# Adaptive max pooling: the short first load as four DMAs

## The chip, the cores and the metric

The kernel runs on 1 core of one Trainium2 chip. The metric is device time in microseconds (us), the median of several runs; lower is better. The profile shows one execution of the program. Its span goes from the first to the last instruction of the core and is shorter than the device time. Engines in the profile: DVE is VectorE, ACT is ScalarE, POOL is GpSimd, SP is SyncE; a letter q behind a name (SPq) means that engine's sequencer, which issues DMAs and waits.

## What is computed

The input x is 32 x 256 x 4096 float32 (134 MB), the output 32 x 256 x 256. Each output is the maximum of 16 neighbouring inputs:

```
for i in range(output_size):          # 256
    start = int(i * length / output_size)
    end = int((i + 1) * length / output_size)
    result[:, :, i] = np.max(x[:, :, start:end], axis=-1)
```

## The kernel before

All windows of 16 inputs form one long list of 2,097,152 windows, 16,384 for each of the 128 partitions. The list is cut into two groups, A and B; in each, a partition owns one contiguous run of windows in HBM, so a load of n windows reads, for each partition, one contiguous row of n x 64 bytes. A load of 1024 windows is 128 rows of 64 KB, 8 MiB in all.

Group A has 10 loads: a short one of 128 windows (FIRST, line 38; 128 rows of 8 KB, 1 MiB), eight of 1024 and one of 1020. Group B has six of 1024 and a last one of 900. All are issued by SyncE, in program order: the short one on line 87, the others on line 96. Within group A the loads go from the end of each partition's run to its start, in group B from start to end.

They land in one buffer, `ring` (line 48), of 2 x (1024 + 152) windows per partition. The short load goes to windows 1024 to 1151. The large loads alternate between the lower and the upper half, and within a half alternately at offset 0 and at offset 152 (GAP). Two loads that follow each other in a half so overlap in all but 152 windows. The reduction of a large load is split accordingly on VectorE (`pooled`, line 54 to 60, called on lines 99 to 101): first a part of 872 windows, which is what the next load in this half overwrites, then the other 152. The next load of the half waits for the first part and is issued while the second part and the other half's load are still going on. The third large load, at windows 152 to 1175 of the lower half, overwrites the short load's place too, so it also waits for the short load's reduction (line 90).

Reductions write into `kept` (line 49), 15,484 windows per partition. The last load's maxima stay in `ring`; ScalarE stores them from there (line 114). SyncE stores the rest in two DMAs behind all the loads (line 117). The framework assigns semaphores and places the waits; each DMA adds to one of eight semaphores in rotation, and a load's reduction waits for that one.

Of the kernel before, what the change touches and what calls it, by code (L numbers as in the profile page):

```python
# [1 line left out]

# [4 lines left out]


@with_exitstack
def kernel(  # L10
    ctx: ExitStack,
    tc: tile.TileContext,
    x: bass.AP,
    output_size: bass.AP,
    out: bass.AP,
):

    nc = tc.nc
    P = nc.NUM_PARTITIONS
    fp32 = mybir.dt.float32

    B, C, L = x.shape
    O = int(output_size)  # L30
    assert L % O == 0, (L, O)
    W = L // O
    total = B * C * O // P
    assert B * C * O % P == 0

    CHUNK = 1024
    GAP = 152
    FIRST = 128
    LOADS_A, LOADS_B = 9, 6

    LESS = 4
    group_a = [FIRST] + [CHUNK] * (LOADS_A - 1) + [CHUNK - LESS]
    last = total - sum(group_a) - LOADS_B * CHUNK
    group_b = [CHUNK] * LOADS_B + [last]
    assert 0 < last and last * (W + 1) <= CHUNK * W

    pool = ctx.enter_context(tc.tile_pool(name="pool", bufs=1))
    ring = pool.tile([P, 2 * (CHUNK + GAP) * W], fp32, tag="ring", name="ring")
    kept = pool.tile([P, total - last], fp32, tag="kept", name="kept")

    xw = x.flatten_outer_dims().rearrange("r (o w) -> (r o) w", w=W)
    ow = out.flatten_outer_dims().rearrange("r o -> (r o)")

    def pooled(dst, at, n):

        nc.vector.reduce_max(  # L56
            out=dst,
            in_=ring[:, at * W : (at + n) * W].rearrange("p (n w) -> p n w", w=W),
            axis=mybir.AxisListType.X,
        )  # L60

    taken = 0

    def group(n):

        nonlocal taken
        span = slice(taken * P, (taken + n) * P)
        taken += n
        return (
            xw[span].rearrange("(p n) w -> p (n w)", p=P),  # L70
            ow[span].rearrange("(p n) -> p n", p=P),
        )

    stores = []
    n_loads = 0
    base = 0
    for g, loads in enumerate((group_a, group_b)):
        xg, og = group(sum(loads))
        a = sum(loads) if g == 0 else 0
        for n in loads:  # L80
            if g == 0:
                a -= n
            xn = xg[:, a * W : (a + n) * W]
            dst = kept[:, base + a : base + a + n] if n != last else None
            if n == FIRST:

                nc.sync.dma_start(  # L87
                    out=ring[:, CHUNK * W : (CHUNK + n) * W], in_=xn
                )
                pooled(dst, CHUNK, n)  # L90
            else:

                low = n_loads % 2 * (CHUNK + GAP)
                moved = n_loads // 2 % 2
                at = low + moved * GAP
                nc.sync.dma_start(out=ring[:, at * W : (at + n) * W], in_=xn)
                if n != last:
                    cut = CHUNK - GAP if moved else GAP
                    parts = [(0, cut), (cut, n)]
                    for u, v in parts if moved else parts[::-1]:  # L100
                        pooled(dst[:, u:v], at + u, v - u)
                else:
                    end = (at + CHUNK) * W
                    last_kept = ring[:, end - n : end]
                    pooled(last_kept, at, n)
                n_loads += 1
            if g:
                a += n
        full = a - last if g else sum(loads)
        stores.append((og[:, 0:full], kept[:, base : base + full]))  # L110
        base += full
    assert taken == total

    nc.scalar.dma_start(out=og[:, full : full + last], in_=last_kept)
    tc.no_sync_barrier()
    for dst, src in stores:
        nc.sync.dma_start(out=dst, in_=src)


# [1 line left out]
_INS = ['x', 'output_size']  # L121
_OUTS = [((32, 256, 256), 'float32')]

_NUMBERS = {'output_size': 256}


# [26 lines left out]
```

## Time and profile before

| what | value |
|---|---|
| device time, median of 3 runs | 335.07 us (334.96 to 335.25) |
| span of the profiled execution | 333.1 us (its own device time is not listed apart; against the median, 2.0 us lie around the span) |
| instructions in the profile | 113 |
| DMA packets, bytes | 2880 packets, 142.61 MB |
| HBM read, written | 134.22 MB, 8.39 MB |
| mean rate over the span | 428 GB/s |
| issue of the short load on SyncE | 0.383 us, from 0.73 us |
| reduction of the short load | 2.29 us, from 5.44 us |
| reduction of 872 windows | 14.69 us each (14 of them) |
| reduction of 152 windows | 2.68 us each (15 of them) |
| reduction of the last load, 900 windows | 15.14 us, from 312.82 us |
| issue of the last store, on ScalarE | at 327.99 us |

How to read it: a DMA is issued by an engine's sequencer, then runs on the core's 16 DMA engines, and lands when all of them have added to its semaphore. A load's packet is one row of a partition (8 KB or 64 KB); besides, each of the 16 engines writes a small end marker per DMA, which counts as a packet too: 19 DMAs on SyncE's queue with 128 rows each make 2432 rows and 304 markers, the 2736 packets that the page gives for that queue. The chain of work goes back from the last instruction, at each step to what released it. The idle time before an instruction is put down to what ended it.

### The profile page before, as it was taken

The numbers are of one execution on the slowest core, as the hardware profiler recorded it, in microseconds if no ns is written. First come the engines' busy times: TensorE is split into PE (matmuls) and PEld (weight loads), VectorE is DVE, ScalarE is ACT, GpSimd is POOL, SyncE is SP. The second block draws the span as 40 slices with busy tenths as digits, with TensorE's granted clock in tenths as the row PEclk, the third lists the DMA queues.
The fourth block names the chain that finished last, engine by engine and source line by source line (L and its number), as shares of the span: only waits on it lengthen the run. The fifth ranks groups of instructions, "written<-read, shape, count | busy, mean of one in ns | idle before, by whom it ended". The sixth has DMA issues, their size and how long they took to land.

```text
span 333.1 us, 113 instructions
## 1 busy us (share of the span) xinstructions
DVE 276.5 (83%) x32; POOL 0.2 (0%) x4
## 2 busy tenths in 40 slices
DVE  2009979797997979799797979979797998979993
POOL 0000000000000000000000000000000000000000
DMA  9898989899898989899898989899898989899997
GB/s 378 378 504 378 504 378 504 378 449 433 378 504 378 504 378 504 378 441 441 384 494 377 504 378 504 378 456 425 386 496 378 504 378 504 378 458 443 393 395 330
DMA packets 2880, 142.61 MB, mean 428 GB/s; under 512 B 320, under 2 KB 320, under 8 KB 448
## 3 DMA queue, kind: packets, MB, share of 16 engines
q1 hardware_dynamic: 2736, 142.15, 98.8%
q10 hardware_dynamic: 144, 0.46, 0.3%
HBM read 134.22 MB, written 8.39 MB: 428 GB/s over the span
## 4 chain that ended last, share of the span: by engine, by line
DMA 57%; DVE 36%; DVEq 5%; issue 0%; SPq 0%
DMA ring<-in_x_dram 57%; DVE kept L56 36%; DVEq L148 5%; SPq L87 0%
## 5 line engine op out<-in xcount | busy, mean ns | idle before, releaser
L56 DVE TENSOR_REDUCE kept<-ring 128x152 f32<-128x2432 f32 (+3 forms) x31 | 261.4, 8473 | 51.5 <-DMA ring<-in_x_dram 51.5
L56 DVE TENSOR_REDUCE ring<-ring 128x900 f32<-128x14400 f32 x1 | 15.1, 15143 | 0.0
L134 POOL MEMSET const-bfloat16-1.0<- 128x1 bf16 x1 | 0.1, 103 | 0.0
L134 POOL MEMSET const-uint8-127<- 128x1 uint8 x1 | 0.1, 102 | 0.0
L134 POOL MEMSET const-float32-0.0<- 128x1 f32 x1 | 0.1, 100 | 0.2 <-issue 0.2
L134 POOL MEMSET const-float32-1.0<- 128x1 f32 x1 | 0.1, 99 | 0.0
## 6 DMA issues: line engine op xcount, KB each, us to landing
ring<-in_x_dram SPq DMA_DIRECT2D x1, 8160.0 KB, 23.9
ring<-in_x_dram SPq DMA_DIRECT2D x1, 7200.0 KB, 21.7
out_dram<-kept SPq DMA_DIRECT2D x1, 4670.0 KB, 32.4
out_dram<-kept SPq DMA_DIRECT2D x1, 3072.0 KB, 18.2
ring<-in_x_dram SPq DMA_DIRECT2D x1, 1024.0 KB, 4.7
out_dram<-ring ACTq DMA_DIRECT2D x1, 450.0 KB, 4.2
ring<-in_x_dram SPq DMA_DIRECT2D x14, 24.0
```

Of the source, the lines that this page charges most:

```text
L56: nc.vector.reduce_max(out=dst, in_=ring[:, at * W : (at + n) * W].rearrange("p (n w) -> p n w", w=W), axis=mybir.AxisListType.X,)
L134: nc = _bacc.Bacc("TRN2", target_bir_lowering=False, num_devices=1)
L148: with _tile.TileContext(nc) as tc:
```

## The change

The short load is no longer one DMA over 128 partitions but four over 32 partitions each, all issued from SyncE one after another. Share s holds the partitions s, s + 4, s + 8 and so on; each row is the same 8 KB from the same address to the same place as before. The reduction of the short load is one instruction as before and waits for all four. The order of instructions on VectorE, ScalarE and GpSimd is unchanged; on SyncE, four DMAs stand where one stood, ahead of all others. The semaphores of the later DMAs shift by three places in their rotation.

```
+    SHARES = 4
...
             if n == FIRST:
 
-                nc.sync.dma_start(
-                    out=ring[:, CHUNK * W : (CHUNK + n) * W], in_=xn
-                )
+                for s in range(SHARES):
+                    nc.sync.dma_start(
+                        out=ring[s:P:SHARES, CHUNK * W : (CHUNK + n) * W],
+                        in_=xn[s:P:SHARES, :],
+                    )
                 pooled(dst, CHUNK, n)
```

## The prediction

> **What bounds the kernel now.** I read the page first, then the chain of work in order of time, SyncE's own waits, and two cuts into stretches: the first microseconds and the end.
>
> The page, busy shares, queues, the chain's shares and the DMA issues:
> ```profile
> DVE 276.5 (83%) x32; POOL 0.2 (0%) x4
> ...
> q1 hardware_dynamic: 2736, 142.15, 98.8%
> ...
> DMA 57%; DVE 36%; DVEq 5%; issue 0%; SPq 0%
> ...
> ring<-in_x_dram SPq DMA_DIRECT2D x1, 1024.0 KB, 4.7
> ```
> VectorE is idle for a sixth of the span, while the 16 DMA engines are taken for 98.8% of it by SyncE's queue. The last line is the load that the change cuts up: 4.7 us from issue to landing.
>
> The chain, from its start (start us, us, what):
> ```profile
> 0.73 0.38 SPq L87
> 1.11 0.05 issue
> 1.16 23.59 DMA ring<-in_x_dram
> 24.76 0.02 issue
> 24.78 14.70 DVE kept L56
> 39.48 0.02 issue
> 39.49 23.96 DMA ring<-in_x_dram
> 63.45 0.02 issue
> 63.48 14.70 DVE kept L56
> ```
> The chain alternates between a load and the reduction that frees its place. It looks like a loop through VectorE, and is not one that decides: the load issued at 39.49 takes 23.96 us, but the load ahead of it lands only at 44.13 (the reduction of it starts there in the timeline). So it stands in the queue for 4.6 us, and the engines never run dry. One 8 MiB load lands every 19.35 us (63.48 - 44.13), that is 433.5 GB/s, and each reduction pair takes 17.28 us, so VectorE then waits 2.07 us for the next landing.
>
> Stretches (us, length, VectorE busy, POOL busy, clock, DMA share, GB/s), the start and then the rest:
> ```profile
> 1.60:1.80 0.20, 0.00 (x0) 0.00 (x0) 1.00 1.63 287
> 1.80:2.00 0.20, 0.00 (x0) 0.00 (x0) 1.00 1.10 205
> 2.00:2.20 0.20, 0.00 (x0) 0.00 (x0) 1.00 0.86 164
> 2.20:2.40 0.20, 0.00 (x0) 0.00 (x0) 1.00 0.20 41
> 2.40:2.60 0.20, 0.00 (x0) 0.00 (x0) 1.00 0.42 123
> 2.60:2.80 0.20, 0.00 (x0) 0.00 (x0) 1.00 0.97 369
> ```
> ```profile
> 0.00:1.60 1.60, 0.00 (x0) 0.20 (x4) 1.00 0.00 0
> 1.60:2.60 1.00, 0.00 (x0) 0.00 (x0) 1.00 0.84 164
> 2.60:4.60 2.00, 0.00 (x0) 0.00 (x0) 1.00 1.01 422
> ...
> 25.00:300.00 275.00, 246.00 (x29) 0.00 (x0) 1.00 1.00 433
> 300.00:312.00 12.00, 12.00 (x2) 0.00 (x0) 1.00 0.94 403
> 312.00:324.00 12.00, 12.00 (x2) 0.00 (x0) 1.00 0.99 425
> 324.00:331.00 7.00, 3.96 (x1) 0.00 (x0) 1.00 0.97 412
> ```
> A packet's bytes are booked where it begins, which is why a short stretch can exceed the engines' rate. The reader is to see three things. Nothing moves before 1.6 us. From 1.6 to 2.6 us only 164 GB/s move. From 2.6 us to 331 us the engines are full, through the stores too: the last store goes out from ScalarE at 328.0 while SyncE's second store still moves until about 330.6. So the time is start + bytes at full rate + a tail, and **any delay or gain in the first 5 us moves the end by as much**, provided the queue doesn't run dry elsewhere.
>
> The change touches just this start. Its time: median 335.07, span of the profiled execution 333.1, so 2.0 us lie around the span; I change neither those nor anything behind 5.1 us.
>
> **The start in detail**, from the trace's packet records. The first load is 128 rows of 8 KB, 8 a DMA engine. In full flow, one such packet follows the other on an engine after 0.306 us (a row of 64 KB after 2.414 us), so a full-rate first load takes 8 x 0.306 = 2.45 us. The first packet begins at 1.75 us, 0.64 after SyncE finished issuing. Fourteen of the engines begin by 2.01, the last visible one at 2.29. The first packets take 0.33 to 1.06 us; from about 2.85 on, all take 0.309. The engines write their end markers (4 bytes, 16 for each DMA) between 4.64 and 5.08. Taking off 2.45, they worked as if started at full rate at 2.19 to 2.63: **the ramp costs the last engine 0.88 us** against 1.75.
>
> **The change, part by part.**
>
> *Issues.* One DMA issue of 0.383 us (start 0.73) becomes four. The next two issues on SyncE took 0.43 and 0.42 and began at 1.16 and 1.64, so I take 0.45 to 0.48 a piece: the shares leave at 0.73, 1.18, 1.65 and 2.12, and the first two 8 MiB loads at about 2.6 and 3.05 in place of 1.16 and 1.64. With the same 1.02 us from issue start to first packet, the first 8 MiB load is ready at about 3.6. The engines need it at 4.2 or later (1.75 + 2.45 at the very earliest). So the 1.4 us of later issue lie beside the first load's own transfer, with 0.6 us of cover. Without that cover it would cost up to 1.4 us, which is a bound.
>
> *Between shares.* Each share has 2 rows an engine, 0.61 us of work, and the next arrives 0.45 to 0.48 later; the queue grows by about 0.15 us per share and doesn't run dry. If an issue of 32 rows takes longer than 0.61 us, it does; nothing in the rows suggests it.
>
> *End markers.* Three more on each engine, 48 in all. In the records, the packet behind a marker starts 6 ns later (4.639 to 4.645), so 3 x 6 = 0.018 us.
>
> *Waits.* The first reduction waits for four landings instead of one. Behind it in VectorE's order stands the reduction of the first 8 MiB load, which waits till 24.76 anyway: 17.05 us of cover. The third 8 MiB load's issue waits for these landings too, but also for the reduction ending at 39.48. Cost 0. All later loads move to other semaphores in a rotation, one wait as before. Cost 0.
>
> *The ramp.* This is the only place where something can be won. Two readings. (a) The slow start is the supply of rows to the engines: 128 rows are handed out over about 0.85 us (1.75 to 2.6), so some engines begin late or stall. A share hands out a quarter, in about 0.21 us, over all engines. Then the last engine works as if from about 2.0 to 2.2 instead of 2.63: a gain of 0.4 to 0.6 us. (b) The slow start is the memory's answer to the first reads: the first rows are as slow in a share, gain 0. Bounds: a gain of 0.88 (no ramp left) plus at most 0.29 if a quarter of the rows took a quarter of the issue's 0.383; below, the loss in the second rival. The staggered starts (1.75 to 2.29) speak for (a); that engines which start at 1.77 still need 1.06 us for a packet speaks for either. I take 0.4, the lower end of (a).
>
> Sum: -0.40 + 0.018 = -0.38 us on 335.07: **334.7**.
>
> [...] The packet behind an end marker starts after 6 ns, and 8 MiB loads land 19.35 us apart at 433.5 GB/s, so back-to-back DMAs leave no hole. [...]
>
> **Rivals.**
>
> 1. *No effect on the ramp* (reading b). The rest costs 0.02 to 0.2 us: **335.1 to 335.3**. For it: the slow packets. Against it: the staggered starts.
>
> 2. *Slower: the shares don't run at full rate.* Every DMA in the trace has 128 rows, dealt 8 to an engine, and runs full. How 32 rows that stand four partitions apart are dealt, no row shows. If only half the engines carry them, or engines meet in pairs at one place of the memory, rows take 2 x 0.306 us, and the first load takes 4.9 us in place of 2.45: +2.45 in full, about +1.2 where engines out of step by over a packet escape it (they end 0.44 us apart now, a packet is 0.306). That is **336.3 to 337.5**. It decides once more than a quarter of the rows (0.67 of 2.45 us) is slowed to half. Against it: one row in four takes in all parts of the partitions evenly.
>
> 3. *Faster by more:* the ramp vanishes and the first packet comes earlier too, -0.7 to -1.1: **334.0 to 334.4**. It needs both bounds nearly in full.
>
> **How the numbers follow.** My forecast (gain of 0.1 to 0.67, 334.4 to 335.0) 0.33; rival 1 0.16; rival 2 0.31; rival 3 0.20. A measurement of this kernel can tell about 0.2%, 0.67 us, from no change: faster means under 334.40, slower over 335.74. So faster 0.20, same 0.49, slower 0.31. The likeliest side alone is 334.4 to 335.4. As the cases of both signs carry over half together, the range takes in the bounds: 334.0 to 337.5.
>
> **What would show it.** Right: 2928 packets (2880 + 48); the first 8 MiB load lands (first big reduction starts) at about 24.4 in place of 24.78; the stretch 1.6 to 2.6 moves clearly more than 164 GB/s; everything behind keeps its 19.35 us spacing. Rival 1: that reduction at 24.8 to 25.0. Rival 2: packets of 8 KB of some 0.6 us, or markers from fewer engines, and the reduction at 26 to 27.2. I would be wrong in another way if the engines idle between shares or before the first 8 MiB load (issue time over 0.61 us), or if a later load loses its 4.6 us of queueing.

## The result and the profile after

The changed kernel is slower: 339.01 us median (338.70 to 339.22) against 335.10 us (334.96 to 335.25), a ratio of 1.0116 with a 95% interval of 1.0104 to 1.0128. That is 3.9 us more, above the upper end of the predicted range (337.5). The profiled execution took 339.22 us, its span 337.4 us.

The page of the changed kernel: busy share of VectorE, packets, SyncE's queue, the issues of the short load's shares (KB each, median us from issue to landing):
```profile
DVE 276.5 (82%) x32; POOL 0.2 (0%) x4
...
DMA packets 2928, 142.61 MB, mean 423 GB/s; under 512 B 368, under 2 KB 368, under 8 KB 496
...
q1 hardware_dynamic: 2784, 142.15, 98.1%
...
ring<-in_x_dram SPq DMA_DIRECT2D x4, 256.0 KB, 3.7
```
Work and bytes are unchanged (276.5 us on VectorE, 142.61 MB); there are the 48 end markers more that were expected. So something waits. The chain from its start (start us, us, what) tells where:
```profile
0.73 0.54 SPq L89
1.27 0.06 issue
1.33 0.57 SPq L89
1.90 0.05 issue
1.95 0.59 SPq L89
2.54 0.04 issue
2.58 0.59 SPq L89
3.17 0.04 issue
3.22 25.45 DMA ring<-in_x_dram
28.67 0.02 issue
28.69 14.70 DVE kept L57
43.39 0.02 issue
43.41 24.27 DMA ring<-in_x_dram
67.68 0.02 issue
67.70 14.70 DVE kept L57
```
Four issues of 0.54 to 0.59 us stand where one of 0.38 stood, 0.60 to 0.64 us from one to the next. The first 8 MiB load is issued at 3.22 us, 2.06 later than before, but its reduction starts at 28.69 instead of 24.78: **3.91 us are lost by the first 8 MiB landing**. Another 0.3 come by 67.70 (4.22 behind), and then the distance holds: the last large pair of reductions starts at 299.86 instead of 295.62 (4.24 behind), and the span is 4.3 longer.

The same stretches of both kernels (us, length, VectorE busy, POOL busy, clock, DMA share, GB/s booked where packets begin). Before:
```profile
2.60:3.60 1.00, 0.00 (x0) 0.00 (x0) 1.00 1.01 418
3.60:4.60 1.00, 0.00 (x0) 0.00 (x0) 1.00 1.00 426
```
Changed:
```profile
1.60:2.60 1.00, 0.00 (x0) 0.00 (x0) 1.00 0.68 131
2.60:3.60 1.00, 0.00 (x0) 0.00 (x0) 1.00 0.93 361
3.60:4.60 1.00, 0.00 (x0) 0.00 (x0) 1.00 0.79 221
4.60:5.60 1.00, 0.00 (x0) 0.00 (x0) 1.00 0.66 246
```
The kernel before is at full rate from 2.6 us on. The changed one reaches 361 GB/s for 1 us and falls back to 221 and 246, about half, from 3.6 us.

The packet records (start, duration and bytes of every packet) show how. In the changed kernel, too, a row of 8 KB in full flow takes 0.309 us; the median over all 128 is the same. But 39 of them take over 0.4 us, against 18 before, and the engines wait. From 3.5 to 9.0 us, on average 12.8 of the 16 have a packet under way, against all 16 before. The first packet begins at 2.05 us instead of 1.75. The end markers of the four shares reach from 2.93 to 3.51, 3.64 to 4.13, 4.51 to 5.31 and 5.39 to 7.42 us: the engines drift apart. The sixteen engines begin their first 64 KB row between 5.73 and 8.60 us; before, between 4.64 and 5.08. The last one is 3.5 us late, and its eight rows then take 19.73 us (to 28.33) instead of 8 x 2.414 = 19.31. These 3.5 and 0.4 are the 3.9 us at the first landing. The reduction of a load starts behind the last of its 16 end markers (28.33 us for the first 8 MiB load, reduction at 28.69; before, 24.40 and 24.78), so the spread of these markers (2.43 us, 0.44 before) counts in full.

One thing in these records is easily missed. The four shares and the first two 8 MiB loads are all issued by 4.28 us. Yet of the 17.6 us that the engines, added up, stand without a packet from 3.5 to 9.0 us, 14.9 lie after 4.28. So most of the waiting is for rows whose DMA has been issued already, and not for an issue.

### The profile page after: what moved, and what is told of

The parts are those of the page before. It is cut to its first block, busy times and chain, and to the rows that moved or that the text cites. A ratio compares the mean times of both kernels' runs of the same rounds, so it can differ in the third digit from the quotient of the medians.

```text
span 337.4 us, 120 instructions
## 1 busy us (share of the span) xinstructions
DVE 276.5 (82%) x32; POOL 0.2 (0%) x4
## 2 busy tenths in 40 slices
DMA packets 2928, 142.61 MB, mean 423 GB/s; under 512 B 368, under 2 KB 368, under 8 KB 496
## 4 chain that ended last, share of the span: by engine, by line
DMA 57%; DVE 36%; DVEq 5%; SPq 1%; issue 0%
DMA ring<-in_x_dram 57%; DVE kept L57 36%; DVEq L151 5%; SPq L89 1%
```

## The experiments

Five kernels were timed once each: the four cuts by windows and the four blocks from SyncE, the load cut in mid-stream, the three tiny DMAs and the step in HBM. The others are medians of 4 to 10. For the scatter: 21 executions of the kernel before lie between 334.75 and 335.63 us.

Three theories after the result. **A**: the engines run dry. A share is 0.61 us of work an engine, the next is issued 0.62 us later, and an engine that has to start anew starts slowly. **B**: the rows of such a share are slow in themselves, because 32 rows four partitions apart are dealt badly to the engines (the second rival of the prediction). **C**: every added DMA has a fixed price, 1.3 us.

### Other cuts of the short load

Four DMAs over all partitions, cut by windows:
```
for s in range(4):
    u = s * n // 4; v = u + n // 4
    nc.sync.dma_start(out=ring[:, (CHUNK + u) * W : (CHUNK + v) * W],
                      in_=xn[:, u * W : v * W])
```


> The short load as four DMAs again, but each over all 128 partitions and 32 windows (rows of 2 KB), all from SyncE. Theory A (the cost is in the issues: four DMAs reach the engines 0.62 us apart, each starting anew, whatever their cut): about as slow as the changed kernel, 338 to 339.5 us, first 8 MiB load landing at 28 to 29 us. Theory B (the cost is in how 32 rows that stand four partitions apart are dealt to the engines, which then hinder one another): 335 to 336.5 us, landing at 24.8 to 26 us.

Measured: 336.37 us, reduction of the first 8 MiB load at 26.23. Theory A's number is missed; the time lies at the upper end of what B was given, the landing just outside. It is 1.3 us slower than before (335.09), not 3.9. What differs at once is the issue. Timeline (start us, us, engine, line):
```profile
0.73 1.81 SPq L90 DMA_DIRECT2D ring<-in_x_dram  x4
```
Four issues in 1.81 us, where the shares modulo 4 take 2.45; each takes 0.38 to 0.43, as in the kernel before.

Four blocks of neighbouring partitions:
```
nc.sync.dma_start(out=ring[32 * s : 32 * s + 32, CHUNK * W : (CHUNK + n) * W],
                  in_=xn[32 * s : 32 * s + 32, :])
```


> The short load as four DMAs of 32 neighbouring partitions each (0 to 31, 32 to 63 and so on). Theory A: 338 to 339.5 us, as the changed kernel. Theory B: the time depends on which partitions a share takes, so it differs from the changed kernel's 339.0 by over 1 us; I would expect it slower, 340 us or more, since a block reaches fewer parts of the memory at a time.

Measured: 336.93 us. A's number is missed. B's general form, a time over 1 us away from 339.0, holds, but the block is faster where B was expected to make it slower. The issues (first line) are short again; the second line is a stretch in which blocks move:
```profile
0.73 1.78 SPq L88 DMA_DIRECT2D ring<-in_x_dram  x4
```
```profile
3.00:6.00 3.00, 0.00 (x0) 0.00 (x0) 1.00 1.04 224
```
It runs at half of the 433.5 GB/s of full flow, its packets of 8 KB take about 0.6 us instead of 0.309. So a cut whose rows are slow in themselves exists, but it is the one into neighbours, not the one modulo 4 (median 0.309 us in the changed kernel).

### The same shares where the queue is full

In mid-stream, one 8 MiB load as shares:
```
if n_loads == 5:
    for s in range(4):
        nc.sync.dma_start(out=ring[s:P:4, at * W : (at + n) * W], in_=xn[s:P:4, :])
```


> The short load whole, as before; one 8 MiB load in mid-stream (the sixth large one) as four shares of 32 partitions modulo 4, rows of 64 KB. Its issues stand behind 4.6 us of queued work. Theory A: the issues are hidden, 335.1 us within 0.4, spacing of landings 19.35 us throughout. Theory B: 8 MiB instead of 1 MiB are dealt in the bad way; at the 207 to 300 GB/s that the changed kernel shows from 4 to 8 us this load takes 28 to 40 us instead of 19.35, so 344 to 356 us.

Measured: 370.54 us, and still not theory B. On SyncE the load that should follow the shares stands ahead of them, and the shares are issued only at 119.45 us, behind a reduction in the other half of the buffer that they need not wait for; the engines stood still from about 102 to 118 and 158 to 174 us. Probably the framework takes a strided slice of partitions for more of the buffer than it covers; no run tests that. As a test of the total it fails. But the shares themselves can be read off, two stretches that each hold one share:
```profile
142.70:147.50 4.80, 0.00 (x0) 0.00 (x0) 1.00 1.01 437
147.50:152.40 4.90, 0.00 (x0) 0.00 (x0) 1.00 0.99 428
```
Shares modulo 4 move at full rate, and their 64 KB rows take 2.418 us, as in any whole load. That speaks against B.

The clean form: 2 MiB ahead of everything, into a part of `kept` that is written late, with the short load once whole and once in four shares.
```
if n == FIRST:
    nc.sync.dma_start(out=kept[:, 11000:15096], in_=xg[:, 0:4096])
    ...
```


> The kernel before with one more DMA ahead of everything on SyncE: 128 rows of 16 KB (2 MiB of x) into columns of kept that late reductions overwrite. It only keeps the engines busy while the short load, whole here, is issued. All theories: 335.1 plus 2.10 MB at 434 GB/s (4.83 us), so 339.9 us within 0.4. It is the base for the next kernel.

> The changed kernel with the same DMA of 2 MiB ahead, so that the four shares (same rows of 8 KB, same partitions modulo 4) are issued while the engines have 4.8 us of work. Theory A (the cost comes from engines that run dry: a share is 0.61 us of work and the next arrives 0.62 us or more later, and each new start is slow): equal to the previous kernel within 0.4 us. Theory B (rows of such shares are slow in themselves): 2 to 4 us above it. Theory C (each added DMA costs a fixed 1.3 us, a third of the 3.9 us): 3.9 us above it.

Measured: 340.00 us (339.92 to 340.21) whole and 339.97 us (339.90 to 340.00) in shares. Timeline of the first, whole:
```profile
1.15 0.42 SPq L89 DMA_DIRECT2D ring<-in_x_dram  x1
...
29.85 17.28 DVE L56 TENSOR_REDUCE kept<-ring 128x872 f32<-128x13952 f32 x2 [17.07 <-DMA ring<-in_x_dram]
```
and of the second, in shares:
```profile
1.16 2.43 SPq L91 DMA_DIRECT2D ring<-in_x_dram  x4
...
29.89 17.28 DVE L57 TENSOR_REDUCE kept<-ring 128x872 f32<-128x13952 f32 x2 [16.97 <-DMA ring<-in_x_dram]
```
The issues take six times as long, and the first 8 MiB load lands at the same time. All 128 packets of 8 KB take 0.309 us in both. **B and C fall; the whole cost goes with the empty queue:** with 4.8 us of work ahead, four shares cost nothing.

### Late issue alone, and faster issue

Three tiny DMAs behind the whole short load:
```
for s in range(1, 4):
    nc.sync.dma_start(out=spare[s:P:4, :], in_=xn[s:P:4, 0:W])
```


> The short load whole, and behind it on SyncE three DMAs of 32 partitions (modulo 4) that load 64 bytes per partition into a tile that nothing reads, so that the first 8 MiB load is issued as late as in the changed kernel, while the 1 MiB goes as before. Theory A in its plain form (late issue of the first 8 MiB load): that load is issued at 2.9 us and ready at about 3.9, the engines end the first load at 4.6 to 5.1, so 335.1 to 335.8 us; if lateness alone is the cost, 337 us or more. Theory B: 335.1 to 335.5 us.

Measured: 335.39 us; the first 8 MiB load is issued at 2.99 us and its reduction starts at 25.14. Lateness of that load and three strided DMAs cost 0.3 us as long as 1 MiB of work lies ahead, where C would have 3.9. The 0.3 us are no idle time. The engines have work throughout, but 13 of the 16 first rows of 64 KB take 2.53 to 2.90 us instead of 2.418.

Two issuers:
```
issuer = nc.scalar if s % 2 else nc.sync
issuer.dma_start(out=ring[s:P:SHARES, ...], in_=xn[s:P:SHARES, :])
```


> The changed kernel with shares 1 and 3 issued from ScalarE, shares 0 and 2 from SyncE, so that all four are out by about 2 us and the first 8 MiB load is issued at about 1.95 us instead of 3.22. Theory A with the issue instruction as what comes too slowly: 335.3 to 337 us. If the hand-over behind the issue is what is too slow, whoever issues: 338 to 339.5 us. Theories B and C: 338.5 to 339.5 us.

> The four DMAs of 32 windows over all 128 partitions (336.37 us from SyncE alone), with the second and fourth issued from ScalarE. If issues that follow one another too slowly are what leaves the engines dry: 335.0 to 335.6 us. If it is not the issues (they were 0.47 us apart, with 0.66 us of work each) but the splitting itself: 336.1 to 336.6 us.

Measured: shares modulo 4 335.84 us (335.60 to 337.35), 0.9 above before (334.96); the four cuts by windows 335.35, 0.4 above. Issuing from two engines takes back 3.0 of 3.9 us, and 0.9 of 1.3. So one issuing engine supplies the DMA engines too slowly. Whether that is the issue instruction, or a hand-over of rows behind it that each issuing engine has for itself, this does not tell; only a hand-over that both share is excluded. The second result is what the first of its two readings expected, although these issues were 0.47 us apart for 0.66 us of work: an interval just below the work is not short enough.

Two parts instead of four:

> Two shares of 64 partitions (modulo 2), 4 rows or 1.22 us of work an engine each. Theory A: the second share arrives 0.6 to 0.9 us behind the first, before the engines are through, so 335.1 to 336.0 us. Theory B (strided partitions): 337 to 339 us. Theory C: one added DMA, 336.4 us.

> The short load as two DMAs of all 128 partitions and 64 windows each (rows of 4 KB), both from SyncE: as many DMAs and as much work each (1.22 us) as with two shares modulo 2, but no step between partitions, so issues of 0.38 to 0.43 us instead of 0.54 to 0.59. If the step between partitions is what made the two shares cost 1.6 us: 335.1 to 335.6 us. If one more DMA at the start costs that whatever its cut: 336.2 to 336.7 us.

Measured: two shares modulo 2 336.53 us (1.6 above before), which is no better than C's number and 0.5 over what A was given; two cuts by windows 335.19 (0.2 above; ratio 1.0008, interval 0.9999 to 1.0017). Same number of DMAs, same work each. The strided ones are issued in 0.55 to 0.58 us, the others in 0.38 to 0.43, and their first packet begins at 2.07 instead of 1.73 us. This left open whether the interval explains all of that or the strided form has a price of its own.

### The work of a share, at the same issues

The 2 MiB (k1) or 4 MiB (k3) ahead as four shares modulo 4, the short load whole behind them; k2 is the base of k3, with the 4 MiB whole:
```
for s in range(4):
    nc.sync.dma_start(out=kept[s:P:4, 11000:15096], in_=xg[s:P:4, 0:4096])
```


> The kernel with 2 MiB ahead (340.0 us with that DMA whole), where the DMA ahead is now cut into four shares modulo 4 with rows of 16 KB, and the short load is whole. Same number of issues at the same 0.62 us as in the changed kernel, but 1.21 us of work a share instead of 0.61. If a share must outlast the interval to the next (dry engines): 0.3 to 1.6 us above 340.0, so 340.3 to 341.6 us. If four strided shares at the start cost 3.9 us whatever their size: 343.9 us.

> As the kernel with 2 MiB ahead, with 4 MiB (rows of 32 KB), whole. 340.0 plus 4.83 us, 344.8 us within 0.4. It is the base for the next.

> The 4 MiB ahead cut into four shares modulo 4, 2.41 us of work a share, issued 0.62 us apart. Dry engines as the cause: only the first packet comes 0.3 us later (2.05 instead of 1.75 us), so 0.2 to 0.6 us above the previous kernel. A price of strided shares whatever their size: 3.9 us above it.

Measured: 341.32 us (k1), 344.92 us (k2), 345.19 us (k3). The issues of k3 (first line) and of k1 (the other two: the shares, then the short load) are as far apart as those of the changed kernel:
```profile
0.72 2.50 SPq L87 DMA_DIRECT2D kept<-in_x_dram  x4
```
```profile
0.72 2.44 SPq L87 DMA_DIRECT2D kept<-in_x_dram  x4
3.21 0.58 SPq L91 DMA_DIRECT2D ring<-in_x_dram  x1
```
With issues about 0.62 us apart, four shares cost:

| work of a share, us an engine | cost against the whole, us |
|---|---|
| 0.61 (the change) | 3.9 |
| 1.21 (k1, against 340.00) | 1.3 |
| 2.41 (k3, against 344.92) | 0.27 |

The last is what the later first packet alone costs (2.04 instead of 1.75 us). So the strided form has no further price once a share is long enough, and the cost falls as the work of a share grows. The interval alone does not set it, though. In k1 a share's work is twice the interval, and so it is in the two shares modulo 2 (1.22 us of work, 0.60 us apart), which cost 1.6 us. In k1 all shares are issued by 3.2 us and the short load by 3.8; yet from 5.0 to 6.0 us on average only 13.9 of the 16 engines have a packet under way, and rows of 16 KB take up to 1.75 us instead of 0.61. The same stretch of the two shares modulo 2 has 14.0. As in the changed kernel, rows come late behind an issue that is done.

Which step lengthens the issue:
```
nc.sync.dma_start(out=ring[32 * s : 32 * s + 32, ...], in_=xn[s:P:4, :])
```


> The four blocks of 32 neighbouring partitions (336.9 us), filled from rows that stand four apart in HBM, so that the short load's rows land in other partitions and the outputs of 128 windows per partition are exchanged among partitions. If the step between SBUF partitions is what lengthens the issue: 0.38 to 0.43 us an issue, as for plain blocks; if a step on either side does: 0.54 to 0.59. If the 8 KB packets of 0.6 us come from the 32 neighbouring partitions written: again 0.6 us and 336.9 us within 0.4; if they come from the neighbouring rows read: 0.31 us and below 336.4 us.

Measured: 337.09 us (the outputs of the short load are left in exchanged partitions; only the times are read), issues as for plain blocks, the first one here:
```profile
0.73 0.39 SPq L88 DMA_DIRECT2D ring<-in_x_dram  x1
```
The median packet of 8 KB takes 0.609 us. So a step in HBM costs the issue nothing, the step between SBUF partitions does (0.54 to 0.59 us in the changed kernel); and the slow packets go with the neighbouring partitions written, not with the rows read.

### Work from another queue meanwhile

The short load issued from ScalarE, whole (r3) and in four shares (r4), SyncE starting with the 8 MiB loads.

> The kernel before, with the short load (whole) issued from ScalarE, so that SyncE issues the first 8 MiB load at 0.73 us instead of 1.16 us and both queues hand rows to the engines from the start. If the slow first microsecond is the hand-over of rows, it shortens: 334.4 to 334.9 us. If it is the memory's answer to the first reads: 335.0 to 335.3 us.

> The changed kernel with all four shares issued from ScalarE, while SyncE issues the first 8 MiB load at 0.73 us. The shares come as slowly as in the changed kernel (0.62 us apart), but the engines have rows of 64 KB from the other queue meanwhile. Theory A (engines that run dry are the cost): within 0.5 us of the previous kernel, so 334.5 to 335.6 us. If the slow issue or the shares cost something apart from dry engines: 336.5 us or more.

Measured: 337.34 and 345.44 us, both far off, for a reason that has nothing to do with dry engines. The DMA engines run full from 5.5 us on in both, but the packet records show one row of 8 KB behind each row of 64 KB: the two queues were taken in turn, packet by packet. The short load so lands last (its 1 MiB took until 24.6 us in r3, 32.2 in r4), and VectorE's reductions are ordered behind it:
```profile
35.12 36.66 DVE L57 TENSOR_REDUCE kept<-ring 128x128 f32<-128x2048 f32 x5 [35.12 <-DMA ring<-in_x_dram]
```
This line is of r4: VectorE starts at 35.12 us instead of 5.44, in r3 at 25.22. As a test of A these two are worthless. They do tell of the start: the first rows of 64 KB take 3.0 to 3.5 us in r4, most of them, instead of 2.418, although both queues were fed at once.

No version beat the kernel before; the nearest is two cuts by windows, the same within 0.2%.

## Why the prediction was wrong

- **What bounds the kernel** was right: a delay in the first 5 us moves the end by as much (3.91 us at the first landing, 4.3 in the span).
- **Issues: failed.** I took 0.45 to 0.48 us a share from the issues of 128 neighbouring partitions. Shares with a step between partitions take 0.54 to 0.59, and 0.60 to 0.64 from one to the next.
- **Between shares: the step that decides, and it failed.** It read that the queue "grows by about 0.15 us per share and doesn't run dry. If an issue of 32 rows takes longer than 0.61 us, it does; nothing in the rows suggests it." The interval did get that long (0.60 to 0.64 us), and engines did run dry. The prediction named this as a way to be wrong, but gave it no chance, and a price (up to 1.4 us) only for the later issue of the 8 MiB loads. A right interval would not have saved the step: 0.47 against 0.66 us of work (cut by windows) still lost 1.3 us, and 0.62 against 1.21 (k1) also 1.3. The step took a DMA's rows as there for the engines 1.02 us after its issue starts; in the changed kernel the first 8 MiB load, issued at 3.22, began its first row at 5.73 and reached its last engine at 8.60.
- **The cover of 0.6 us for the first 8 MiB load: failed.** I had it ready at 3.6 us. Its last engine begins it at 8.60.
- **The ramp: failed.** The gain of 0.4 us did not come; the first packet came 0.3 later, and the slow start, which I had hoped to shorten, came again: rows of the second and third share take up to 0.88 us. The number of reading (b), no gain from smaller portions, fits better: starts from idle are as slow with rows of 64 KB (0.6 to 1.1 us over 2.418 for most, in r4). Its cause, the memory's answer to first reads, no run shows.
- **End markers, waits, packet count:** right (2928 packets; no wait of VectorE or of a later load became the bound).
- **Rival 2** (slow rows, 336.3 to 337.5 us) had the right sign, and its mechanism was not the one: shares modulo 4 ran at full rate where the queue was full (428 and 437 GB/s). Its ceiling of 2.45 us assumed slow rows in 1 MiB only. The real loss also takes in engines that drift apart and start late on the next load.

What stays open: why a dry engine gets its next rows so late (up to 8.60 us for a load issued by 3.8), and why the rows that it holds then run slowly for a while (each engine's first 64 KB row took 2.81 to 3.36 us instead of 2.418). The runs show that both vanish with 4.8 us of queued work (all 16 first rows take 2.418 us in both kernels with 2 MiB ahead), not what causes them. Slow rows also came without a dry engine, in the kernel with three tiny DMAs (2.53 to 2.90 us for 13 of the 16 first rows).

## What to carry to other kernels

In this kernel, cutting a DMA into parts was free with 4.8 us of work in the queue, and dear at a cold start: there a part had to outlast the interval to the next issue several times over (2.4 us of work for 0.62 us made it 0.3 us; twice the interval 1.3; equal 3.9). Before cutting by partitions, take the issue's duration from the very form that will be issued; a step between SBUF partitions made it 0.16 us longer. If one must cut at a start, cutting by columns over all partitions was cheaper (0.2 us for two parts, 1.3 for four), and so was issuing from two engines (0.9 us for the four shares, 0.4 for four cuts by columns).

## What the runs showed of the hardware

- A DMA with a step between SBUF partitions (2 or 4) took 0.52 to 0.62 us to issue from SyncE, where one without took 0.37 to 0.43 at the start of the kernel, and the first plain DMA behind it took long too (0.58 to 0.59). As the first DMA of a kernel, its first packet came 0.3 us later (2.05 us in the changed kernel, 1.75 before). A step in HBM cost the issue nothing (0.39 and 0.41 us, one execution).
- Rows to 32 neighbouring partitions moved at 224 GB/s, rows to 32 partitions four apart at 428 to 437 with a full queue.
- The DMA engines took SyncE's and ScalarE's queue in turn by packets, not by bytes: beside rows of 64 KB, the short load's 1 MiB took until 24.6 us when whole (r3) and 32.2 us in shares (r4). With VectorE's reductions ordered behind the short load, the kernel became 2.4 us (r3) and 10.5 us (r4) slower.
